# Seven products in place of eight for four of 22 gate and up blocks of a feed-forward stage

## The chip, the cores and the metric

The kernel runs on one core of a Trainium2 chip, whose engines work side by side: TensorE (PE, with its weight loads shown as PEld) multiplies, VectorE (DVE) and ScalarE (ACT) work on elements, GpSimd (POOL) is nearly unused here, SyncE (SP) issues the loads. The metric is device microseconds for one execution; lower is better. Every execution computes the whole of the reference from arrays in the chip's main memory.

## The reference

Two layers over 256 tokens with 1024 features, float32. Each layer is a feed-forward stage, a mixing stage and a second feed-forward stage, each added to x. So there are four feed-forward stages, which are what the change is about:

```python
def swiglu(h, w_gate_up, w_down):
    a, b = jnp.split(h @ w_gate_up, 2, axis=-1)
    return (jax.nn.silu(a) * b) @ w_down

x = x + 0.5 * swiglu(rms_norm(x, ffn1_norm), ffn1_w_gate_up, ffn1_w_down)
h = rms_norm(x, mix_norm)
# mixing: pooling over windows of 2, 4, 8, 16 tokens and causal attention, gated and merged
x = x + merged @ w_out
x = x + 0.5 * swiglu(rms_norm(x, ffn2_norm), ffn2_w_gate_up, ffn2_w_down)
```

The hidden width is 2816, 22 blocks of 128 features. w_gate_up has 1024 rows and 5632 columns, w_down 2816 rows and 1024 columns. rms_norm multiplies each token by one factor (the reciprocal root of its mean square) and each feature by a gain.

## The kernel before

**Precision.** Every float32 operand is split into two float32r parts, hi (a rounded copy, made by ScalarE) and lo (the rest, made by VectorE). A product is hi x hi, hi x lo and lo x hi, added up in PSUM. With the activations as the moving operand, one matmul streams 512 columns (hi and lo of 256 tokens) past the hi weights, and a second streams the 256 hi columns past the lo weights: `chain` (L136). Where the weights move and the activations stand (`tokens`, L369, for q, k and v in the mixing stage), a k-step of 128 rows is four matmuls of 512, 256, 512 and 256 columns.

**Weights.** They arrive in units of 1 MB, 128 partitions x 2048 columns. `fetch` (L96) loads one into a "raw" tile (four buffers) through SyncE's queue and splits it in two halves of 1024 columns into "hi" and "lo" tiles (six buffers each, so three units); `unit` (L90) hands the oldest one out. A gate and up unit holds one block of 128 gate features and the matching 128 up features, for all eight k-blocks of 128 rows: unit[p, k, gate or up, 128].

**A feed-forward stage** (`ffn`, L296). The gain is multiplied into x while it is split (`split_x`, L224, into "hx"); the factor per token is computed beside the first blocks (`factor_spread`, L276) and multiplied in later. For each of 22 blocks `pair` (L154) runs 8 x 2 chains into a PSUM tile of the pool "mm" (two buffers), then `drain` adds the two column halves (one copy on ScalarE, one add on VectorE) into "ab". A block or more later "ab" is scaled by the token factor (L340, VectorE), ScalarE takes the Silu of the gate half (L344), VectorE multiplies (L345), and `halves` (L187) splits the result into the tiles "ga", "gc" and "gb" (8, 8 and 6 blocks). Then comes the down projection: eight output blocks, each with 22 chains over those tiles into a PSUM tile of the pool "at" (four buffers; L347 to L359), added to x by `add_x`.

**Order.** TensorE runs in the order in which the program is written (`mm` wraps every matmul with `keep`, L78). The other engines' instructions are put in order by a planner, which takes them by their place in the program as soon as their operands and buffers are free; `behind` (L169) pins one behind another. Each engine then runs its own instructions strictly in that order.

The first stage of the first layer starts while its weights still arrive and has its own code (`n0`); the other three take the `else` branch at L320. In the mixing stage the tiles "gc" and "gb" hold other things (L482 to L488).

Of the kernel before, what the change touches and what calls it, by code (L numbers as in the profile page):

```python
# [18 lines left out]
F32 = mybir.dt.float32  # L19
# [23 lines left out]


C_G1, C_GM, C_G2, C_BG, C_PS, NG = 0, 8, 16, 24, 40, 44


@with_exitstack
def trunk_kernel(ctx: ExitStack, tc: tile.TileContext, x_in, w_in, pw_in, qkn_in, rope_in, mask_in, band_in, out):
# [28 lines left out]
    def mm(*args, **kw):  # L78
        return keep(nc.tensor.matmul(*args, **kw))  # L79
# [5 lines left out]

    n_unit = [0]

    ahead = []

    def unit():  # L90

        if not ahead:
            fetch()
        return ahead.pop(0)

    def fetch(last=None):  # L96

        raw, hi, lo = buffers()
        u = n_unit[0]
        n_unit[0] += 1  # L100
        n = HALF if u < 4 else 2 * HALF
        for c in range(0, 2 * HALF, n):
            nc.sync.dma_start(raw[:, c:c + n], w_in[u, :, c:c + n])
# [6 lines left out]
    def buffers():  # L110
        raw = raws.tile([P, 2 * HALF], F32, name="raw", tag="raw")
# [19 lines left out]

    def prod(ps, w, xk, first, last):

        return mm(steps(ps), lhsT=w, rhs=steps(xk), start=first, stop=last)

# [80 lines left out]
    for t in range(PAD - 1):  # L216
        g = min(g for g, w in enumerate(WINDOWS) if t < w - 1)
        nc.gpsimd.memset(inv[:, g:, t:t + 1], 1.0 / (t + 1))

    hx = acts.tile([P, NK, 2, S], F32R, name="hx")  # L220
    hk = [hx[:, k] for k in range(NK)]
# [45 lines left out]
    def spread(dr, st):  # L267
# [6 lines left out]
        return r  # L274

    def factor_spread():  # L276

# [17 lines left out]

    def ffn(after, n0=0, end=False):  # L296
        gs = []
        for n, m in (("ga", 8), ("gc", 8), ("gb", NF - 16)):
            g = acts.tile([P, m, 2, S], F32R, name=n, tag=n)
            gs.extend(g[:, i] for i in range(m))  # L300
        abs_ = []

        def wide():
            if n0 and len(abs_) in range(5, 13):
                ab = acts.tile([P, 2, S], F32, name="ab", tag="gates", bufs=NK)
            else:
                ab = tmp.tile([P, 2, S], F32, name="ab", tag="t512", bufs=5)
            abs_.append((len(abs_), ab))
            return abs_[-1][1]

        r = []

        def sums():
            r.append(factor_spread())

        if n0:
            pairs([unit() for _ in range(n0)], [wide() for _ in range(n0)])
            pair(unit(), wide(), sums, NK // 2)
            fetch()
        else:  # L320
            ws = [unit() for _ in range(2)]
            ts = [wide() for _ in range(2)]
# [3 lines left out]
            drain(ts[0], pss[0])  # L326
            sums()
            columns(ws[1], pss[1], range(4, NK))
            drain(ts[1], pss[1])
        done = 0  # L330
        for i in range(n0 + 1 if n0 else 2, NF + 1):
            if i < NF:
                pair(unit(), wide())
                fetch()

            todo = range(done, min(done + (2 if not n0 or i % 3 == 2 else 1), i) if i < NF else NF)
            done = todo.stop
            for j in todo:
                ab = abs_[j][1]
                scaled = tt(ab, ab, bc2(r[0]), op=OP.mult)  # L340
# [3 lines left out]
                act(sg, ab[:, 0, :], AF.Silu)  # L344
                tt(sg, sg, ab[:, 1, :], op=OP.mult)  # L345
                halves(gs[j], sg)
        for b in range(NK * NF):  # L347
# [129 lines left out]
    def mix(l, after):  # L477
# [7 lines left out]
        spare = acts.tile([P, 8 * GW], F32, name="spare", tag="ga")  # L485
        ax = acts.tile([P, 8, 2, S], F32R, name="ax", tag="gc")
        yk, pk = ([ax[:, i] for i in range(a, a + 4)] for a in (0, 4))
        qk = acts.tile([P, 12, S], F32, name="qk", tag="gb")  # L488
# [229 lines left out]
    for f in range(NK):  # L718
        square_x(f)
    n_unit[0] = len(w3)  # L720
    ahead.extend(w[1:] for w in w3)
    for l in range(L):
        ffn(lambda f: prep(f, l, C_GM), len(w3) if l == 0 else 0)
        if l == 0:
            for d, z in ((rope, rope_in), (mask, mask_in), (qkn, qkn_in)):
                nc.sync.dma_start(d, z)
        mix(l, lambda f: prep(f, l, C_G2))
        if l + 1 < L:
            ffn(lambda f: prep(f, l + 1, C_G1))
        else:  # L730
            ffn(lambda f: nc.sync.dma_start(out[:, f, :], x[:, f, :]), end=True)

# [89 lines left out]
```

## Time and profile before

| What | Value |
|---|---|
| Runs | 1004.05 us (median of 3: 1003.82, 1004.05, 1006.15) |
| Span of the profiled execution | 1001.7 us; the page states no time of its own for it |
| TensorE, matmuls | 996.8 us busy |
| VectorE, ScalarE | 788.9 and 619.0 us busy |
| Granted TensorE clock | 1.00 of full speed in all 40 slices |
| Loads | 192.89 MB, mean 193 GB/s |

The span runs from the first to the last instruction; a run's time has some more around it. A row of a group reads: line of the code, engine, operation, output tile and input tiles, shape, count, busy time and mean ns of one, then the idle time of that engine just ahead of these instructions and what ended it. A row of the chain reads: start, duration, engine and tile, number of instructions. The three stages that the change touches begin at 326, 502 and 822 us of the span (48 matmuls of 0.167 us ahead of the factor's "ss" matmuls at 334.25, 510.50 and 829.89).

### The profile page before, as it was taken

The page shows a single profiled execution, that of the slowest core. Times are in us where ns is not written, and L with a number is a line of the kernel's source. Part 1 is how long each engine was busy: PE and PEld are TensorE (multiplying, and loading weights), DVE is VectorE, ACT ScalarE, POOL GpSimd, SP SyncE. Part 2 cuts the span into 40 slices and gives each one's busy share as a digit, 9 for nine tenths or more (in the row PEclk, how much of TensorE's full clock was granted, in tenths as well). Part 3 has the DMA queues.
Part 4 walks back from the last instruction along what each step waited for, and adds up shares of the span by engine and source line. Part 5 has one row for each costly group of instructions (what it writes and reads, how often), then busy time and mean ns, then how long its engine had stood idle before and what let it go on. Part 6 is the DMA issues. An engine that isn't in the chain of part 4 may idle for free.

```text
span 1001.7 us, 16029 instructions
## 1 busy us (share of the span) xinstructions
PE 996.8 (100%) x6348; PEld 905.8 (90%) x6348; DVE 788.9 (79%) x1175; ACT 619.0 (62%) x981; POOL 16.1 (2%) x46
## 2 busy tenths in 40 slices
PE   9999999999999999999999999999999999999998
PEld 8899888898899988999988888889989999989988
DVE  6998866698978888886688888666988888888752
ACT  7866655557756666665576666556677567666541
POOL 0000000002000000000000000000020000000000
PEclk9999999999999999999999999999999999999999
DMA  8866655643546665565556566555544465565640
GB/s 290 318 210 210 210 183 196 220 156 137 187 152 211 208 212 173 206 210 191 192 189 213 183 209 203 185 202 190 185 178 171 134 215 202 190 203 196 207 150 22
DMA packets 30170, 192.89 MB, mean 193 GB/s; under 512 B 3344, under 2 KB 4624, under 8 KB 7568
## 3 DMA queue, kind: packets, MB, share of 16 engines
q1 hardware_dynamic: 30096, 191.88, 55.8%
q8 instruction: 49, 0.80, 0.3%
q14 instruction: 25, 0.20, 0.1%
HBM read 190.82 MB, written 1.05 MB: 192 GB/s over the span
## 4 chain that ended last, share of the span: by engine, by line
PE 99%; DMA 0%; DVE 0%; ACT 0%; SPq 0%; issue 0%
PE ps L79 84%; PE pt L79 7%; PE two L79 4%; PE pe L79 1%; PE sc L79 1%; PE pt L463 1%; PE y L79 1%; DMA raw<-w 0%; PE tp L419 0%; PE st L79 0%; PE ss L79 0%; DVE gx L367 0%; ACT hi L117 0%; SPq L708 0%
## 5 line engine op out<-in xcount | busy, mean ns | idle before, releaser
L79 PE MATMUL ps<-hx,hi 128*128 128x512 f32 x1696 | 568.5, 383 | 0.5 <-ACT hi L117 0.5
L118 DVE TENSOR_TENSOR lo<-raw,hi 128x1024 fp32r<-128x1024 f32 (+2 forms) x372 | 441.1, 1192 | 137.9 <-ACT hi L117 133.1
L117 ACT ACTIVATE hi<-raw 128x1024 fp32r<-128x1024 f32 (+2 forms) x372 | 380.8, 1030 | 230.4 <-PE ps L79 175.8
L79 PE MATMUL ps<-hx,lo 128*128 128x256 f32 x1696 | 463.4, 273 | 0.0
L79 PEld LDWEIGHTS ps<-hx,hi 128*128 128x128 f32 x1696 | 318.4, 188 | 57.6 <-ACT hi L117 0.8
L79 PEld LDWEIGHTS ps<-hx,lo 128*128 128x128 f32 x1696 | 318.7, 188 | 0.2 <-DVE lo L118 0.2
L79 PE MATMUL ps<-ga,hi 128*128 128x512 f32 (+1 forms) x264 | 87.0, 376 | 0.0
L79 PE MATMUL ps<-gc,hi 128*128 128x512 f32 (+1 forms) x264 | 87.0, 376 | 0.0
L79 PE MATMUL ps<-ga,lo 128*128 128x256 f32 x256 | 69.9, 273 | 0.0
L79 PE MATMUL ps<-gc,lo 128*128 128x256 f32 x256 | 69.9, 273 | 0.0
L79 PE MATMUL ps<-gb,hi 128*128 128x512 f32 (+1 forms) x198 | 65.6, 376 | 0.0
L79 PE MATMUL pt<-hi,hx 128*128 128x512 f32 x192 | 64.9, 384 | 0.0
L340 DVE TENSOR_TENSOR ab<-ab,r 128x512 f32<-128x512 f32 x88 | 60.3, 690 | 2.2
L167 DVE TENSOR_TENSOR ab<-ps,ab 128x512 f32<-128x512 f32 x86 | 59.0, 686 | 2.0
L79 PEld LDWEIGHTS ps<-ga,hi 128*128 128x128 f32 x264 | 49.0, 188 | 8.3
L79 PEld LDWEIGHTS ps<-gc,hi 128*128 128x128 f32 x264 | 49.0, 188 | 8.3
L79 PE MATMUL pt<-lo,hx 128*128 128x256 f32 x192 | 52.5, 274 | 0.0
L344 ACT ACTIVATE sg<-ab 128x256 f32<-128x256 f32 x88 | 36.2, 417 | 26.4 <-DVE ab L340 24.8
L79 PE MATMUL ps<-gb,lo 128*128 128x256 f32 x192 | 52.4, 273 | 0.0
L166 ACT ACTIVATE ab<-ps 128x512 f32<-128x512 f32 x86 | 49.9, 580 | 0.0
L79 PEld LDWEIGHTS ps<-gc,lo 128*128 128x128 f32 x256 | 48.1, 188 | 0.0
L79 PEld LDWEIGHTS ps<-ga,lo 128*128 128x128 f32 x256 | 48.1, 188 | 0.0
(150 smaller groups left out, 1018.9 us busy)
## 6 DMA issues: line engine op xcount, KB each, us to landing
raw<-w SPq DMA_DIRECT2D x176, 1024.0 KB, 5.0
raw<-w SPq DMA_DIRECT2D x16, 256.0 KB, 5.3
out_dram<-gx SPq DMA_DIRECT2D x8, 128.0 KB, 2.0
gx<-x SPq DMA_DIRECT2D x3, 256.0 KB, 6.3
qk<-pw SPq DMA_DIRECT2D x2, 256.0 KB, 2.7
gx<-x SPq DMA_DIRECT2D x1, 300.0 KB, 2.9
qkn<-qkn SPq DMA_DIRECT2D x1, 256.0 KB, 5.2
rope<-rope SPq DMA_DIRECT2D x1, 128.0 KB, 5.0
```

The lines of the kernel that those rows point to most:

```text
L79: return keep(nc.tensor.matmul(*args, **kw))
L117: act(hi, w, AF.Copy)
L118: return tt(lo, w, hi.bitcast(F32), op=OP.subtract)
L166: act(t, ps[:, :, 1, :], AF.Copy)
L167: drained.append(tt(t, ps[:, :, 0, :], t, op=OP.add))
L340: scaled = tt(ab, ab, bc2(r[0]), op=OP.mult)
L344: act(sg, ab[:, 0, :], AF.Silu)
L463: keep(nc.tensor.transpose(pt[:, h, o * P:(o + 1) * P], pr[:, h, c * P:(c + 1) * P], ident))
```

## The change

Blocks 12 to 15 of three feed-forward stages are no longer multiplied one by one. Their 256 gate and up columns each make a matrix of 1024 columns, cut in two by two blocks: W11 and W12 (rows 0 to 511; blocks 12, 13 and blocks 14, 15), W21 and W22 (rows 512 to 1023). The activations with the gain are cut in two by two as well, by 128 tokens and by 512 features. The four result blocks then come from seven products of (128 tokens x 512) by (512 x 512) in place of eight, by a scheme of Strassen's kind.

- The order of weights is a list, `feed_order`: blocks 0 to 4, then one of the seven forms ahead of each of the blocks 5 to 11, then blocks 16 to 21.
- `sum_form` makes a form of the weights. Forms 1, 2 and 3 are plain loads (W11 into the tile "sa", W21 into a raw tile, W22 into a part of the tile "pre"). Forms 5, 6 and 4 add W12, W22 and W21 to "sa" in turn, and form 7 adds W12 to "pre": these four are loads that add, issued by GpSimd. Each form is 1 MB and is split like a unit.
- `x_forms`, behind the drain of block 2, makes four sums of the activations and splits them; three products take parts of "hx" as they are.
- `by_tokens` multiplies: activations stand, weights move, four matmuls per k-step as in `tokens`. The result has tokens on the partitions.
- `strassen` sums the products and gates them (`gated`), with the token factor as a scalar per partition; `factor_tokens` computes it so at the stage's start, from two matmuls of one column.
- `turned` transposes the gated blocks on TensorE, two blocks of features at a time, behind blocks 11 and 16, and splits them into the tile "gd", which takes half of what was "gc".

Nothing changes in the first stage, the down projection and the mixing stage, but that "gc" is now two tiles there too.

```diff
+GROUP = 12
+FIRST = 5
+FORMS = {
+    "1": ("a", False, "11"), "2": ("c", False, "21"), "5": ("a", True, "12"), "3": ("b", False, "22"),
+    "6": ("a", True, "22"), "7": ("b", True, "12"), "4": ("a", True, "21"),
+}
+def feed_order():
+    z, forms = [], list(FORMS)
+    for n in (*range(GROUP), *range(GROUP + 4, NF)):
+        if n >= FIRST and forms:
+            z.append(forms.pop(0))
+        z.append(n)
+    return z
+def feed_units(base):
+    return [base + n if isinstance(n, int) else (base, n) for n in feed_order()]
...
+    plan = []
+    for base in (0, FU, LU, LU + FU):
+        plan.extend(feed_units(base) if base else range(NF))
+        plan.extend(range(base + NF, base + NF + NF // 2))
+        if base in (0, LU):
+            plan.extend(range(base + NF + NF // 2, base + FU))
...
+        u = next(plan)
+        if isinstance(u, tuple):
+            ahead.append(sum_form(*u))
...
+    def sum_form(base, f):
+        n = base + GROUP
+        q = {"11": (n, 0), "12": (n + 2, 0), "21": (n, 1), "22": (n + 2, 1)}
+        at, add, src = FORMS[f]
+        if at == "c":
+            sums_at["c"] = raws.tile([P, 2 * HALF], F32, name="raw", tag="raw")
+        z = sums_at[at].rearrange("p (i c) -> p i c", i=2)
+        u, kh = q[src]
+        w = w_in[u:u + 2, :, kh * HALF:(kh + 1) * HALF].rearrange("u p c -> p u c")
+        if add:
+            nc.gpsimd.dma_start(z, w, accum_op=OP.add)
+        else:
+            nc.sync.dma_start(z, w)
+        _, hi, lo = buffers(False)
+        z = z.rearrange("p i (k c) -> p i k c", c=2 * P)
+        for h in range(2):
+            a = z[:, :, 2 * h:2 * h + 2, :]
+            hv, lv = (t[h].rearrange("p (k i c) -> p i k c", i=2, c=2 * P) for t in (hi, lo))
+            act(hv, a, AF.Copy)
+            tt(lv, a, hv.bitcast(F32), op=OP.subtract)
+        return hi, lo
...
+    def factor_tokens():
+        st = quarter("st")[:, 0, :2]
+        for t in range(2):
+            mm(st[:, t:t + 1], lhsT=acc[:, t * P:(t + 1) * P], rhs=ones[:, :1], start=True, stop=True)
+        rt = small.tile([P, 2], F32, name="rt", tag="rt", bufs=2)
+        rsqrt(rt, st, 1.0 / D)
+        nt = small.tile([P, 2], F32, name="nt", tag="nt", bufs=1)
+        nc.vector.tensor_scalar(nt, rt, -1.0, None, op0=OP.mult)
+        return rt, nt
...
+        def post(n):
+            ab = abs_[n]
+            scaled = tt(ab, ab, bc2(r[0]), op=OP.mult)
+            sg = small.tile([P, S], F32, name="sg", tag="sg", bufs=2)
+            act(sg, ab[:, 0, :], AF.Silu)
+            tt(sg, sg, ab[:, 1, :], op=OP.mult)
+            halves(gs[n], sg)
+            return scaled
...
+            sums_at["a"] = acts.tile([P, 2 * HALF], F32, name="sa", tag="gd")
+            pre = acts.tile([P, 12 * S], F32, name="pre", tag="gb")
+            sums_at["b"] = pre[:, :NK * S]
+            xg = pre[:, :NK * S].rearrange("p (k s) -> p k s", s=S)
+            vt = acts.tile([P, 2, GW], F32, name="vt", tag="v")
+            tk = [acts.tile([P, 2, GW], F32, name="tk", tag="tok", bufs=2) for _ in range(2)]
+            p1, p5, c12 = tk[0][:, 0], tk[0][:, 1], tk[1][:, 0]
+            gq = {tn: vt[:, tn // 2, tn % 2 * S:(tn % 2 + 1) * S] for tn in range(4)}
+            sf = {}
+            def x_forms():
+                late = drained[-1]
+                for k in range(NK):
+                    behind(act(xg[:, k, :], x[:, k, :], AF.Copy, scale=gain[:, l_of[0], col + k:col + k + 1]), late)
+                a11, a21 = (xg[:, :4, t * P:(t + 1) * P] for t in range(2))
+                a12, a22 = (xg[:, 4:, t * P:(t + 1) * P] for t in range(2))
+                s1, s2 = (pre[:, (8 + 2 * i) * S:(10 + 2 * i) * S].rearrange("p (k s) -> p k s", s=P) for i in range(2))
+                s3, s4 = (vt[:, i, :].rearrange("p (k s) -> p k s", s=P) for i in range(2))
+                tt(s1, a22, a21, op=OP.subtract)
+                stt(s2, s1, -1.0, a11, op0=OP.mult, op1=OP.subtract)
+                tt(s3, a11, a21, op=OP.subtract)
+                stt(s4, s2, -1.0, a12, op0=OP.mult, op1=OP.subtract)
+                for n, z in (("5", s1), ("3", s4), ("6", s2), ("7", s3)):
+                    sh, sl = (acts.tile([P, 4, P], F32R, name="sf", tag="gates", bufs=NK) for _ in range(2))
+                    act(sh, z, AF.Copy)
+                    tt(sl, z, sh.bitcast(F32), op=OP.subtract)
+                    sf[n] = [(sh[:, k, :], sl[:, k, :]) for k in range(4)]
+                for n, k0, t in (("1", 0, 0), ("2", 4, 0), ("4", 4, 1)):
+                    sf[n] = [tuple(hx[:, k, j, t * P:(t + 1) * P] for j in range(2)) for k in range(k0, k0 + 4)]
+            def by_tokens(f, ps, first):
+                hi, lo = unit()
+                more = {} if first else {"skip_group_check": True}
+                for k, (ah, al) in enumerate(sf[f]):
+                    wh, wl = blk(hi, 4 * k, 4), blk(lo, 4 * k, 4)
+                    prod(ps, ah, wh, first and k == 0, False, **more)
+                    prod(ps[:, :S], ah, wl[:, :S], False, False, **more)
+                    prod(ps, al, wh, False, False, **more)
+                    prod(ps[:, S:], ah, wl[:, S:], False, k == 3, **more)
                 fetch()
-            todo = range(done, min(done + (2 if not n0 or i % 3 == 2 else 1), i) if i < NF else NF)
-            done = todo.stop
-            for j in todo:
-                ab = abs_[j][1]
-                scaled = tt(ab, ab, bc2(r[0]), op=OP.mult)
-                if n0 and i == n0 + 1:
-                    behind(scaled, drained[-1])
+            def gated(c, t, n, sign):
+                c = c.rearrange("p (i j s) -> p i j s", i=2, j=2)
+                sc = r[1][sign][:, t:t + 1]
                 sg = small.tile([P, S], F32, name="sg", tag="sg", bufs=2)
-                act(sg, ab[:, 0, :], AF.Silu)
-                tt(sg, sg, ab[:, 1, :], op=OP.mult)
-                halves(gs[j], sg)
+                act(by_half(sg), c[:, :, 0, :], AF.Silu, scale=sc)
+                stt(by_half(gq[2 * t + n]), c[:, :, 1, :], sc, by_half(sg), op0=OP.mult, op1=OP.mult)
+            def turned(n):
+                pt = quarter("pt")
+                for i in range(2):
+                    for t in range(2):
+                        keep(nc.tensor.transpose(pt[:, i, t * P:(t + 1) * P], gq[2 * t + n][:, i * P:(i + 1) * P], ident))
+                g = gt[2][:, 2 * n:2 + 2 * n]
+                act(g[:, :, 0, :], pt, AF.Copy)
+                tt(g[:, :, 1, :], pt, g[:, :, 0, :].bitcast(F32), op=OP.subtract)
+            bank = {}
+            def strassen(f):
+                b = {"1": "a", "2": "a", "5": "e", "3": "e", "6": "g", "7": "f", "4": "f"}[f]
+                fresh = b not in bank
+                if fresh:
+                    bank[b] = quarter("p" + b).rearrange("p a s -> p (a s)")
+                z = bank[b]
+                by_tokens(f, z, fresh)
+                if f == "1":
+                    act(p1, z, AF.Copy)
+                elif f == "2":
+                    gated(z, 0, 0, 0)
+                elif f == "5":
+                    act(p5, z, AF.Copy)
+                elif f == "6":
+                    tt(p1, z, p1, op=OP.add)
+                    tt(c12, bank["e"], p1, op=OP.add)
+                    gated(c12, 0, 1, 1)
+                elif f == "7":
+                    tt(p5, z, p5, op=OP.add)
+                    tt(p5, p5, p1, op=OP.add)
+                    gated(p5, 1, 1, 1)
+                elif f == "4":
+                    tt(p1, z, p1, op=OP.add)
+                    gated(p1, 1, 0, 0)
+            late = []
+            wait = [0, 1]
+            for i, n in enumerate(feed_order()[2:]):
+                if isinstance(n, str):
+                    strassen(n)
+                    if n in "74":
+                        late.append([2, 1 if n == "7" else 0])
+                    continue
+                pair(unit(), wide(n))
+                fetch()
+                if i == 0:
+                    x_forms()
+                for m in wait[:2]:
+                    post(m)
+                wait = wait[2:] + [n]
+                if n == GROUP - 1:
+                    room("gd", 4)
+                    room("gb", NF - 16)
+                for z in late:
+                    z[0] -= 1
+                    if z[0] == 0:
+                        turned(z[1])
+            for m in wait:
+                post(m)
         for b in range(NK * NF):
             f, k = divmod(b, NF)
             if b % 16 == 0:
...
```

More of the change, by code (lines that the diff above doesn't have):

```diff
@@ L108, in fetch, with buffers @@
         ahead.append((hi, lo))
-    def buffers():
-        raw = raws.tile([P, 2 * HALF], F32, name="raw", tag="raw")
+    sums_at = {}
+    def sum_form(base, f):
[19 more added lines that the diff above has]
+        return hi, lo
+    def buffers(raw=True):
+        raw = raws.tile([P, 2 * HALF], F32, name="raw", tag="raw") if raw else None
         hi = [parts.tile([P, HALF], F32R, name="hi", tag="hi") for _ in range(2)]
@@ L130, in steps, with prod @@
         return z.rearrange("p (s a c) -> p a s c", a=4, c=4)
-    def prod(ps, w, xk, first, last):
-        return mm(steps(ps), lhsT=w, rhs=steps(xk), start=first, stop=last)
+    def prod(ps, w, xk, first, last, **kw):
+        return mm(steps(ps), lhsT=w, rhs=steps(xk), start=first, stop=last, **kw)
     def chain(ps, hi, lo, b, xk, first, last):
@@ L294, in bc2, with ffn, room, wide @@
         return a.unsqueeze(1).to_broadcast([P, 2, a.shape[-1]])
-    def ffn(after, n0=0, end=False):
-        gs = []
-        for n, m in (("ga", 8), ("gc", 8), ("gb", NF - 16)):
+    def ffn(after, n0=0, end=False, col=None):
+        gs, gt = [], []
+        def room(n, m):
             g = acts.tile([P, m, 2, S], F32R, name=n, tag=n)
+            gt.append(g)
             gs.extend(g[:, i] for i in range(m))
-        abs_ = []
-        def wide():
+        room("ga", 8)
+        room("gc", 4)
+        abs_ = {}
+        def wide(n):
             if n0 and len(abs_) in range(5, 13):
-                ab = acts.tile([P, 2, S], F32, name="ab", tag="gates", bufs=NK)
+                abs_[n] = acts.tile([P, 2, S], F32, name="ab", tag="gates", bufs=NK)
             else:
-                ab = tmp.tile([P, 2, S], F32, name="ab", tag="t512", bufs=5)
-            abs_.append((len(abs_), ab))
-            return abs_[-1][1]
+                abs_[n] = tmp.tile([P, 2, S], F32, name="ab", tag="t512", bufs=5)
+            return abs_[n]
         r = []
@@ L314, in sums @@
             r.append(factor_spread())
-        if n0:
-            pairs([unit() for _ in range(n0)], [wide() for _ in range(n0)])
-            pair(unit(), wide(), sums, NK // 2)
-            fetch()
+            if not n0:
+                r.append(factor_tokens())
+        def post(n):
[6 more added lines that the diff above has]
+            return scaled
+        if n0:
+            room("gd", 4)
+            room("gb", NF - 16)
+            ws = [unit() for _ in range(n0)]
+            pairs(ws, [wide(n) for n in range(n0)])
+            pair(unit(), wide(n0), sums, NK // 2)
+            fetch()
+            done = 0
+            for i in range(n0 + 1, NF + 1):
+                if i < NF:
+                    pair(unit(), wide(i))
+                    fetch()
+                todo = range(done, min(done + (2 if i % 3 == 2 else 1), i) if i < NF else NF)
+                done = todo.stop
+                for n in todo:
+                    scaled = post(n)
+                    if i == n0 + 1:
+                        behind(scaled, drained[-1])
         else:
             ws = [unit() for _ in range(2)]
-            ts = [wide() for _ in range(2)]
             pss = [banks(pmm, "ps") for _ in range(2)]
@@ L485, in mix @@
         spare = acts.tile([P, 8 * GW], F32, name="spare", tag="ga")
-        ax = acts.tile([P, 8, 2, S], F32R, name="ax", tag="gc")
-        yk, pk = ([ax[:, i] for i in range(a, a + 4)] for a in (0, 4))
+        yk, pk = ([z[:, i] for i in range(4)] for z in (
+            acts.tile([P, 4, 2, S], F32R, name=n, tag=t) for n, t in (("yk", "gc"), ("pk", "gd"))))
         qk = acts.tile([P, 12, S], F32, name="qk", tag="gb")
@@ L719, in trunk_kernel @@
         square_x(f)
-    n_unit[0] = len(w3)
+    for _ in w3:
+        next(plan)
     ahead.extend(w[1:] for w in w3)
     for l in range(L):
-        ffn(lambda f: prep(f, l, C_GM), len(w3) if l == 0 else 0)
+        l_of[0] = l
+        ffn(lambda f: prep(f, l, C_GM), len(w3) if l == 0 else 0, col=C_G1)
         if l == 0:
```

23 lines of the change are left out of this document (12 added, 11 removed).

## The prediction

> **What bounds the kernel now.** I read the page's busy line first, then the chain of waits in order of time, then the groups of one stretch, and last the queues. The busy line and the chain's summary:
>
> ```profile
> PE 996.8 (100%) x6348; PEld 905.8 (90%) x6348; DVE 788.9 (79%) x1175; ACT 619.0 (62%) x981; POOL 16.1 (2%) x46
> PE 99%; DMA 0%; DVE 0%; ACT 0%; SPq 0%; issue 0%
> ```
>
> TensorE sets the end: the chain never leaves it for longer than the first load. So time comes off only where TensorE gets fewer columns, and any wait put ahead of a matmul is paid in full. The chain in order of time gives what a matmul costs (start, us, what, how many):
>
> ```profile
> 182.86 10.96 PE pt L79 x64
> 193.82 0.34 PE st L79 x4
> 194.16 10.78 PE pt L79 x64
> 204.94 0.34 PE st L79 x2
> 205.28 10.68 PE pt L79 x64
> 215.96 0.87 PE tp L419 x8
> 216.83 10.67 PE ps L79 x64
> ...
> 334.25 0.23 PE ss L79 x2
> 334.47 176.02 PE ps L79 x1056
> ```
>
> The last row is a whole feed-forward stage without a gap: 1056 matmuls in 176.02 us, 166.7 ns each (a 512-column and a 256-column one alternate). A gate and up block is 16 pairs, so 32 x 0.1667 = 5.33 us. The row starts in the middle of block 1 (the "ss" matmuls stand there), so block 1 ends at 334.47 + 16 x 0.1667 = 337.14, block 4 at 353.1, block 6 at 363.8.
>
> How near VectorE and ScalarE are to a bound is read in the same stage, blocks 4 to 21 (window, length, busy of PE, PEld, DVE, ACT, POOL, clock, DMA share, GB/s; then VectorE's and ScalarE's groups there):
>
> ```profile
> 350.00:446.00 96.00, 96.00 (x578) 86.38 (x577) 80.43 (x111) 59.96 (x90) 0.00 (x0) 1.00 0.59 200
> ```
> ```profile
> L118 DVE TENSOR_TENSOR lo<-raw,hi 128x1024 fp32r<-128x1024 f32 x37 | 45.3, 1223 | 10.9 <-ACT hi L117 9.8
> L167 DVE TENSOR_TENSOR ab<-ps,ab 128x512 f32<-128x512 f32 x19 | 13.0, 687 | 0.6
> L340 DVE TENSOR_TENSOR ab<-ab,r 128x512 f32<-128x512 f32 x18 | 12.4, 692 | 0.6
> L345 DVE TENSOR_TENSOR sg<-sg,ab 128x256 f32<-128x256 f32 x18 | 7.5, 418 | 0.0
> ...
> ```
> ```profile
> L117 ACT ACTIVATE hi<-raw 128x1024 fp32r<-128x1024 f32 x36 | 38.0, 1054 | 19.1 <-PE ps L79 19.1
> L166 ACT ACTIVATE ab<-ps 128x512 f32<-128x512 f32 x18 | 10.4, 580 | 0.0
> L344 ACT ACTIVATE sg<-ab 128x256 f32<-128x256 f32 x18 | 7.6, 420 | 5.7 <-DVE ab L340 5.6
> ...
> ```
>
> 96 us are 18 blocks: VectorE works 80.43 / 18 = 4.47 us of each 5.33, ScalarE 3.33. VectorE is the second engine, with 0.86 us to spare per block; ScalarE waits for TensorE to give weight buffers back (19.1 us), so splits run as far ahead as the buffers allow. How far, by VectorE's and ScalarE's timelines:
>
> ```profile
> 350.42 1.06 ACT L117 ACTIVATE hi<-raw 128x1024 fp32r<-128x1024 f32 x1 [0.82 <-PE ps L79]
> ```
> ```profile
> 350.93 0.68 DVE L340 TENSOR_TENSOR ab<-ab,r 128x512 f32<-128x512 f32 x1
> 351.53 1.22 DVE L118 TENSOR_TENSOR lo<-raw,hi 128x1024 fp32r<-128x1024 f32 x1
> ```
>
> At 350.42 block 4's first half has just been used up. Three units fit the buffers, so this split is for block 7, which starts at 363.8: it is done at 352.75, a **lead** of 11.0 us.
>
> **The change part by part.** All terms are per stage, three stages.
>
> Products. Removed: four blocks, 128 matmuls, 128 x 0.1667 = 21.33 us. Added: seven products of 4 k-steps with 2 x (512 + 256) columns, 112 matmuls in the form that "pt" has (activations stationary, weights moving). The trace has that form at 10.96, 10.78 and 10.68 us for 64, mean 10.81 or 168.9 ns each: 112 x 0.1689 = 18.91 us. **Gain 2.42 us**; with 10.96 (19.18 for 112) it is 2.15, with the "ps" rate of 10.67 (18.67) it is 2.66. I take the mean, the three rows being the same code with the same operands as the products.
>
> Added on TensorE: eight 128x128 transposes ("turned"), 0.87 us by the "tp" row, and two one-column matmuls with the scale per token ("factor_tokens"), 0.34 us by the "st" x4 row. Both stand in TensorE's program order, so nothing covers them: **loss 1.21 us**. The transposes come two blocks after their product (at least 5.33 + 5.33 us behind it), and what they wait for (two sums, a Silu, a multiplication) is below 3 us of work by the 0.69 and 0.42 us groups, so I cost that wait at nothing; without the cover it would be those 3 us.
>
> Net on TensorE 2.42 - 1.21 = 1.21 us per stage, 3.6 us in all.
>
> VectorE and ScalarE. The four blocks lose their drains and gating, but seven forms are split in place of four units. Over the stretch in which a form stands ahead of each of blocks 5 to 11, TensorE takes 7 x 5.33 + 18.91 = 56.2 us. VectorE needs 7 x 4.47, plus 7 forms x 2 x 1.223, plus five 512-wide sums at 0.69 and four 256-wide multiplications at 0.42 from the "strassen" branches: 31.3 + 17.1 + 5.1 = 53.5 us. It fits, with 2.7 us left. But "x_forms" comes before it, behind the drain of block 2: eight 512-wide operations at 0.69 (5.5 us), and five tiny ones of the scale per token (the tiny ones of the token scale last 0.16 each):
>
> ```profile
> L252 DVE SCALAR_TENSOR_TENSOR rt<-a,rt 128x2 f32<-128x2 f32 x2 | 0.3, 161 | 0.1
> ```
>
> That is 6.3 us, against 3 x 0.86 = 2.6 to spare in blocks 2 to 4: the stretch begins 3.7 us late on VectorE. With a form between blocks, three units of buffers are worth 5.33 - 2.7 = 2.6 us less, so the lead is 11.0 - 2.6 = 8.4 us. 3.7 is below 8.4: **I cost it at nothing, hidden by the lead**, and with the lead gone it would be 3.7 us per stage. ScalarE: x_forms adds eight 256-wide scaled copies (the split of the activations shows 0.50) and four 512-wide (0.58), 6.3 us, against 3 x 2.0 spare; in the stretch 7 x (3.33 + 2.11) + 2 x 0.58 + 4 x 0.42 = 40.9 of 56.2.
>
> ```profile
> L227 ACT ACTIVATE hx<-gx 128x256 fp32r<-128x256 f32 x48 | 23.6, 499 | 6.8 <-DVE gx L367 3.6 <-DVE gx L696 1.7 <-DMA gx<-x 1.3
> ```
>
> PSUM. A second product of a bank waits until the first was read out (form 2 behind the copy of 1, form 3 behind that of 5, form 4 behind the sum of 7). A block of 5.33 us stands between each two; the copy takes 0.58, the sum 0.69. Nothing, unless the queue of that engine is 4.6 us late.
>
> Loads. Seven 1 MB transfers replace four; four of them add into a tile and come from GpSimd's queue, which is idle in these stages. SyncE's queue:
>
> ```profile
> SPq L103 <- DVE lo L118: 540.5, 117, 16.2
> SPq L103 <- DVE sg L345: 218.3, 34, 6.5
> ```
> ```profile
> raw<-w SPq DMA_DIRECT2D x176, 1024.0 KB, 5.0
> ```
> ```profile
> DMA to landing us min/median/max: 4.1/5.0/10.5
> ```
>
> SyncE waits for buffers, not for memory. Two new waits stand in it: form 1 waits until the tile "gd" is free of the stage before, form 3 until x_forms has read "pre"; the block loads behind each wait too. A load is issued when the raw tile four units before has been split, some 6 units before its use, and by its landing of 5.0 us (10.5 at worst) it has over 15 us in hand: nothing. Form 5 waits, on GpSimd, for the split of form 1 (both use tile "sa"), 6 for 5, 4 for 6. Between two uses of the tile stand two blocks and two forms, 16.1 us of TensorE; the split itself takes 1.05 + 2 x 1.22 = 3.5, so an adding load has 12.6 us before it delays a split, and the lead on top. The trace has no adding load. From below it is a plain one, 5.0; from above, one that moves its bytes twice through what the others leave: 0.59 of the engines carry 200 GB/s, so all carry 339, and the other 0.41 carry 139; 2.1 MB at 139 GB/s are 15.1 us, and 1.9 of start and landing (5.0 less 1.05 MB at 339) make 17.0. I take a value below 12.6, as the nearest row is the plain load: nothing.
>
> [...]
>
> **Sum:** span 1001.7 less 3.6 is 998.1. The page gives no time of its own for the profiled execution; the runs' median, 1004.05, lies 2.35 above the span, so the forecast is **1000.4 us**. Its own range goes by the product rate: gain 2.15 gives 3 x 0.94 = 2.8 and 1001.2, gain 2.66 gives 3 x 1.45 = 4.4 and 999.7.
>
> **The rivals.**
>
> A, small stalls take the gain. The lo half waits for the hi half of the same weights (9.8 us of waits in the window above), so the two engines' lateness may add instead of overlap: ScalarE's 6.3 us of x_forms ahead of the next hi half and VectorE's 3.7 behind it make 10.0 against a lead of 8.4, 1.6 us per stage, 4.8 in all: 1005.2; with half of it 1002.8. For it: both engines get their extra work at one place. Against: the splits of the next two units are already done when it starts. It would be within 0.3%.
>
> B, slower: the adding loads are late. Three follow each other on one tile; with 17.0 us each is 4.4 late, together 13.2, less the lead of 8.4, 4.8 us per stage: 1000.4 + 14.4 = 1014.8. It decides from 12.6 + 8.4 / 3 = 15.4 us per load. For it: the 10.5 us worst plain load, and that ScalarE, waiting for the load, keeps the drains of finished blocks behind it. Against: GpSimd and 0.41 of the DMA engines are free.
>
> C, slower: VectorE becomes the bound in the stretch. In the window it idles 96 - 80.4 = 15.6 us, over 18 units 0.87 each. If this idle time belongs to each split, the 14 units of the stretch need 53.5 + 12.2 = 65.7 us for TensorE's 56.2; 9.5 + 3.7 - 8.4 = 4.8 per stage: 1014.8 too. Against: the idle time is there because the buffers are full, and goes when VectorE is behind.
>
> D, the change doesn't gain what it says: all products at the slowest "pt" rate or a little slower, and the waits of the transposes not covered by 0.5 us a stage: 1001.2 + 1.5 = 1002.7, within 0.3%.
>
> **How the numbers follow.** A measurement of this kernel can tell 0.3%, 3.0 us, from no change: faster is below 1001.0, slower above 1007.1. Forecast 0.44, A 0.22, D 0.08, B 0.12, C 0.14. Faster 0.45 (forecast, and a little of A with stalls near nothing), same 0.30, slower 0.25. The range goes from 999.2 (the forecast's lower end, less half of the three 0.34 us, since the "st" row also holds the change to the next tile) up to 1010: it holds the forecast, A, D and the small half of B and C (stalls of half the worked size, 1007.6). The forecast's own range is 999.7 to 1001.2.
>
> **What would show it.** In the changed kernel's chain: per stage 128 matmuls less of "ps" and 112 more of the new form; a stage with 1.2 us less from its "ss" row to the next stage's; eight transposes at 0.87. Right: TensorE's busy share stays at 99 to 100% and its waits stay below 1 us. A shows as waits of TensorE for hi or lo of the units just behind x_forms. B shows as ScalarE waiting for a transfer at the splits of forms 5, 6, 7, 4, and landing times above 15 us. C shows as VectorE at 95% or more from block 5 to 11 and TensorE waiting for lo. D shows as more than 169 ns per matmul of the products. Wrong altogether: a TensorE clock below 1.00, or stalls in stages that have no products.

## The result and the profile after

The changed kernel takes 1010.21 us (median of 6 runs, 1007.77 to 1013.67) beside 1003.93 us for the kernel before (6 runs, 1003.43 to 1006.15): a ratio of 1.0063, 95% interval 1.0043 to 1.0082. It is 0.6% slower where 0.4% faster was forecast. The profiled execution took 1010.54 us, with a span of 1008.8. The six runs of the changed kernel lie 5.9 us apart, at mean granted TensorE clocks of 0.997 to 1.000 that do not put them in order.

The busy line and the summary of the chain, from the page of the changed kernel:

```profile
PE 997.2 (99%) x6336; PEld 904.4 (90%) x6336; DVE 808.9 (80%) x1217; ACT 641.5 (64%) x1026; POOL 30.6 (3%) x58
PE 81%; DMA 9%; DVE 4%; ACT 3%; issue 2%; SPq 0%; ACTq 0%; POOLq 0%
```

No engine is overloaded on average; VectorE rose from 79% to 80%. But the chain (the work that ended last, followed back step by step), which was TensorE alone before, now runs 9% of the span through DMA, and through VectorE and ScalarE behind it. Where it leaves TensorE is read in the chain in order of time (start, us, what):

```profile
334.73 0.34 PE st L103 x4
335.07 18.79 PE ps L103 x112
...
353.91 8.95 DMA sa<-w
...
369.67 10.99 DMA sa<-w
...
384.83 12.48 DMA sa<-w
...
397.42 1.06 ACT hi L163
...
404.12 0.61 DVE tk L510
...
404.87 4.57 PE pf L103 x16
409.44 5.47 PE ps L103 x32
414.91 0.44 PE pt L484 x4
...
584.16 2.92 PE pf L103 x16
...
905.27 2.90 PE pf L103 x16
```

(The row of 112 at 335.07 is the rest of block 1 and blocks 2 to 4; the 112 matmuls of the products come after it.) In the first and the third changed stage the chain goes through the three adding loads of tile "sa" (forms 5, 6 and 4), in the second through form 5's and then that of "pre" (form 7). From there it goes through ScalarE and VectorE, and in all three it comes back to TensorE at product 4 ("pf"). The groups of waits of the whole execution (us in total, times, longest) say what stood still:

```profile
ACT hi L163 <- DMA sa<-w: 26.9, 9, 3.7
ACT hi L163 <- DMA pre<-w: 9.7, 3, 4.3
PE pf L103 <- DVE tk L510: 6.2, 3, 2.4
```

ScalarE waited 36.6 us for the twelve adding loads, 12.2 per stage, and TensorE waited once per stage, 2.4 us at most, for the sum "tk" of product 7. The loads themselves (KB each, us to landing; L155 issues the POOLq ones):

```profile
raw<-w SPq DMA_DIRECT2D x167, 1024.0 KB, 4.9
sa<-w POOLq DMA_DIRECT2D x9, 1024.0 KB, 10.0
pre<-w POOLq DMA_DIRECT2D x3, 1024.0 KB, 13.0
```

How a wait of ScalarE becomes one of TensorE is seen in the two timelines of the first such place (start, us, engine, line, what; in brackets the idle time ahead and what ended it). ScalarE's:

```profile
397.42 1.06 ACT L163 ACTIVATE hi<-sa 128x1024 fp32r<-128x1024 f32 x1 [3.32 <-DMA sa<-w]
...
400.09 1.05 ACT L163 ACTIVATE hi<-sa 128x1024 fp32r<-128x1024 f32 x1
401.04 0.57 ACT L223 ACTIVATE ab<-ps 128x512 f32<-128x512 f32 x1
```

VectorE's:

```profile
399.65 1.22 DVE L164 TENSOR_TENSOR lo<-sa,hi 128x1024 fp32r<-128x1024 f32 x1
...
401.17 1.23 DVE L164 TENSOR_TENSOR lo<-sa,hi 128x1024 fp32r<-128x1024 f32 x1
402.31 0.68 DVE L224 TENSOR_TENSOR ab<-ps,ab 128x512 f32<-128x512 f32 x1
402.91 1.21 DVE L175 TENSOR_TENSOR lo<-raw,hi 128x1024 fp32r<-128x1024 f32 x1
404.04 0.68 DVE L510 TENSOR_TENSOR tk<-pf,tk 128x512 f32<-128x512 f32 x1
```

Product 7 ended on TensorE at 396.93, so its sum (L510) could have run then. In VectorE's order it stands behind both lo halves of form 4, the drain of block 9 (which had ended at 394.18) and another lo half. The lo halves need ScalarE's hi halves, and these wait for the load. So the sum runs at 404.04, 7.1 us after its operands were there. Product 4 accumulates into the same PSUM bank and may not start before the sum has read it; between product 7 and product 4 stands one block of 5.35 us. 7.1 less (5.35 - 0.68) is 2.4 us, and that is the gap in the trace: TensorE has nothing from 402.43 to 404.87. In the other two stages it is 1.8 and 1.9 us. Form 4 itself was there in time.

The longest gap cost more than its length. The stretch behind it (window, length, busy of PE, PEld, DVE, ACT and POOL, clock, DMA share, GB/s):

```profile
402.50:409.28 6.78, 4.41 (x16) 3.83 (x17) 6.78 (x10) 4.51 (x8) 0.00 (x0) 0.75 0.18 37
```

The granted clock is 0.75 there, and product 4 took 4.57 us; behind the gaps of 1.8 and 1.9 it took 2.92 and 2.90. The three gaps make 6.2 us, the slow product 1.7 more: 7.9 us, about the distance from the changed kernel to the versions below that have no gap (1001.7 to 1002.5).

### The profile page after: what moved, and what is told of

It is laid out like the page before. It is cut to its first block, busy times and chain, and to the rows that moved or that the text cites. A ratio compares the mean times of both kernels' runs of the same rounds, so it can differ in the third digit from the quotient of the medians.

```text
span 1008.8 us, 16140 instructions
## 1 busy us (share of the span) xinstructions
PE 997.2 (99%) x6336; PEld 904.4 (90%) x6336; DVE 808.9 (80%) x1217; ACT 641.5 (64%) x1026; POOL 30.6 (3%) x58
## 4 chain that ended last, share of the span: by engine, by line
PE 81%; DMA 9%; DVE 4%; ACT 3%; issue 2%; SPq 0%; ACTq 0%; POOLq 0%
PE ps L103 65%; DMA sa<-w 7%; PE pt L103 7%; PE two L103 4%; DVE lo L164 1%; DMA pre<-w 1%; PE pe L103 1%; DVE lo L175 1%; PE pf L103 1%; PE sc L103 1%; ACT hi L163 1%; ACT pre L442 1%; PE pt L657 1%; DVE ab L224 1%; PE y L103 1%
## 5 line engine op out<-in xcount | busy, mean ns | idle before, releaser
L103 PE MATMUL ps<-hx,hi 128*128 128x512 f32 x1504 | 506.9, 384 | 0.9 <-ACT hi L174 0.9
L175 DVE TENSOR_TENSOR lo<-raw,hi 128x1024 fp32r<-128x1024 f32 (+2 forms) x348 | 411.1, 1189 | 111.5 <-ACT hi L174 109.2
L174 ACT ACTIVATE hi<-raw 128x1024 fp32r<-128x1024 f32 (+2 forms) x348 | 352.8, 1026 | 180.0 <-PE ps L103 128.5
L103 PE MATMUL ps<-hx,lo 128*128 128x256 f32 x1504 | 411.0, 273 | 0.0
L103 PEld LDWEIGHTS ps<-hx,hi 128*128 128x128 f32 x1504 | 282.4, 188 | 51.8 <-ACT hi L174 1.2
L103 PEld LDWEIGHTS ps<-hx,lo 128*128 128x128 f32 x1504 | 282.6, 188 | 0.3 <-DVE lo L175 0.3
L163 ACT ACTIVATE hi<-sa 128x1024 fp32r<-128x1024 f32 x24 | 25.3, 1052 | 30.3 <-DMA sa<-w 26.9
L103 PE MATMUL ps<-gc,hi 128*128 128x512 f32 (+1 forms) x132 | 44.3, 376 | 0.0
L103 PE MATMUL ps<-gd,hi 128*128 128x512 f32 (+1 forms) x132 | 44.3, 376 | 0.0
L103 PE MATMUL ps<-mk,hi 128*128 128x256 f32 x256 | 44.1, 275 | 0.0
```

What stands on the lines that cost most here:

```text
L163: act(hv, a, AF.Copy)
L174: act(hi, w, AF.Copy)
L175: return tt(lo, w, hi.bitcast(F32), op=OP.subtract)
```

## The experiments

What had to be explained was the wait of product 4, and that even without it the time would stand at 1002, not 1000.4. Theory 1 was formed from the trace after: the adding loads land in 8.4 to 13.9 us, ScalarE stands still at the split that waits for them, and the drains and sums behind that split in the in-order queues of ScalarE and VectorE come late. Its rivals: that the order in which the planner laid these queues is the cause and the loads are only what it is stretched by; that the extra work of `x_forms` had used up the lead, whatever the loads do; and that GpSimd's queue, not the addition, makes the loads slow. The ratios are to the kernel before, run beside each of them.

**Loads that do not add.**

```diff
         if add:
-            nc.gpsimd.dma_start(z, w, accum_op=OP.add)
+            nc.gpsimd.dma_start(z, w)
```

> The four adding loads per stage are issued as plain loads, same queue, same tile, same order of instructions on every engine; the weights of forms 5, 6, 7 and 4 are then single quarters, not sums, so the output is not the reference's. Theory 1 (the adding loads land 9 to 13 us after their issue, ScalarE stands still for them in its fixed order, and everything behind it gets late): landings near 5 us, ScalarE's wait for these loads falls from 12.6 us in the first changed stage to under 3, TensorE's wait for the sum of product 7 (6.2 us in three stages) is gone, time about 1002 us. Rival 2 (the order alone puts that sum too late, whatever the loads do): the wait stays at 2 us per stage, time 1007 to 1010. Rival 3 (the work of x_forms puts both engines behind): also 1007 to 1010.

Measured 1002.24 us (11 runs) beside 1003.81 (29 runs): 0.9983 (0.9974 to 0.9992). The five engines have the same instructions in the same order as the changed kernel. From its page and its waits:

```profile
sa<-w POOLq DMA_DIRECT2D x9, 1024.0 KB, 5.7
pre<-w POOLq DMA_DIRECT2D x3, 1024.0 KB, 5.5
```

```profile
ACT hi L163 <- DMA sa<-w: 1.8, 2, 1.5
```

The same bytes from the same queue land in 5.7 and 5.5 us instead of 10.0 and 13.0, ScalarE's 36.6 us of waiting become 1.8, and TensorE's wait is gone. So the addition makes the loads long, not the queue; and with the order unchanged, short loads suffice to remove the stall.

**The same loads, another order.** The first split of an adding form is pinned behind the drain of an earlier block.

```diff
-            act(hv, a, AF.Copy)
+            first = act(hv, a, AF.Copy)
+            if add and h == 0:
+                behind(first, drained[-2])
```

> Only the order is changed: the first half split of each form that is made by an adding load is put behind the drain of the block that is two blocks back. Theory 1: the loads still land 9 to 13 us after issue, but fewer instructions stand behind the wait; TensorE's wait for the sum of product 7 goes below 1 us per stage, time 1002 to 1004. Rival 2: the wait is gone as well, 1002 to 1004. Rival 3: the wait stays, 1007 to 1010.

Measured 1001.90 us (9 runs): 0.9977 (0.9967 to 0.9986). The loads land in 11.6 and 13.0 us, no sooner than before, but ScalarE waits for them 12.0 us in place of 36.6, in shorter pieces:

```profile
ACT hi L163 <- DMA sa<-w: 8.7, 7, 2.1
ACT hi L163 <- DMA pre<-w: 3.3, 3, 1.5
```

VectorE's timeline at the same place shows the sum of product 7 between the two lo halves of form 4, 6 us sooner than in the changed kernel:

```profile
396.73 1.23 DVE L166 TENSOR_TENSOR lo<-sa,hi 128x1024 fp32r<-128x1024 f32 x1
397.87 0.68 DVE L512 TENSOR_TENSOR tk<-pf,tk 128x512 f32<-128x512 f32 x1
398.47 1.22 DVE L166 TENSOR_TENSOR lo<-sa,hi 128x1024 fp32r<-128x1024 f32 x1
```

TensorE doesn't wait. Long loads alone are no stall either; they need an order that puts a drain or a sum behind the wait.

**Without x_forms.** Its sums and splits are left out; products 5, 3, 6 and 7 multiply parts of "hx".

```diff
                 if i == 0:
-                    x_forms()
+                    for fm, k0, t in (("1", 0, 0), ("2", 4, 0), ("4", 4, 1), ("5", 0, 1), ("3", 4, 0), ("6", 0, 0), ("7", 4, 1)):
+                        sf[fm] = [tuple(hx[:, k, j, t * P:(t + 1) * P] for j in range(2)) for k in range(k0, k0 + 4)]
```

> x_forms is left out: no sums of the activations are made, products 5, 3, 6 and 7 take parts of hx in their place, so the output is not the reference's. Adding loads as in the changed kernel. Rival 3: no backlog, TensorE's wait gone, 1001 to 1003, and ScalarE no longer waits for the adding loads. Theory 1: the first adding load is issued some 5 us sooner (348 in place of 353.9 us of the first changed stage), but each still lands 9 to 13 us after issue and ScalarE waits for it, 6 us per stage or more; TensorE's wait for the sum of product 7 is smaller than 2 us per stage but the time stays above 1003. Rival 2: 1007 to 1010.

Measured 1001.73 us (11 runs): 0.9978 (0.9969 to 0.9986). The stall is gone here too, with loads of 11.0 and 11.1 us:

```profile
ACT hi L163 <- DMA sa<-w: 6.5, 4, 3.3
ACT hi L163 <- DMA pre<-w: 1.5, 2, 0.8
```

Theory 1 had expected more than 1003. So the loads are not enough by themselves: without the work of x_forms (on VectorE 345.75 to 354.7 in the changed kernel, eight operations between the usual ones) the splits are earlier and the first adding load is issued at 349.84 in place of 353.91. The planner also lays the queues anew when the work is gone, and that part is not separated.

**Form 4's splits behind the sum of product 7, on both engines.**

```diff
+            first = act(hv, a, AF.Copy)
+            low = tt(lv, a, hv.bitcast(F32), op=OP.subtract)
+            if f == "4" and h == 0:
+                behind(first, sum7[-1])
+                behind(low, sum7[-1])
```

> Only the order is changed: the split of form 4 stands behind the sum of product 7 on ScalarE and VectorE. Rival 2: TensorE's wait is gone, 1002 to 1003. Theory 1: the sum is no longer behind the wait for the last load, but the split of form 4 now comes later and TensorE waits for hi or lo of form 4 instead, 1 to 2 us per stage, time 1005 to 1010.

Measured 1006.82 us (9 runs): 1.0026 (1.0016 to 1.0035). The wait for the sum is gone, and TensorE waits for the lo halves of form 4 themselves:

```profile
PE pf L103 <- DVE lo L165: 1.9, 2, 1.0
```

So putting the sum ahead by itself passes part of the stall on to the split: 1006.82 is still 4.6 us above the kernel with plain loads, where the changed kernel is 8.0 above it. What repairs it is the place of every adding form's split, as in the order above.

**The work of x_forms twice, with plain loads, and with the pinned order.** The sums and the splits of x_forms run twice; the first kernel has loads that do not add, the second the pinned order with adding loads.

```diff
-                tt(s1, a22, a21, op=OP.subtract)
...
+                for _ in range(2):
+                    tt(s1, a22, a21, op=OP.subtract)
...
-                    act(sh, z, AF.Copy)
-                    tt(sl, z, sh.bitcast(F32), op=OP.subtract)
+                    for _ in range(2):
+                        act(sh, z, AF.Copy)
+                        tt(sl, z, sh.bitcast(F32), op=OP.subtract)
```

> Plain loads in place of the adding ones, and the sums and splits of x_forms are made twice: 5.5 us more on VectorE and 2.3 us more on ScalarE at the place of x_forms in each stage. The weights of forms 5, 6, 7 and 4 are single quarters, so the output is not the reference's. Theory 1 (lateness of the two sources adds up, and the adding loads are the larger part): twice the work alone stays below the lead, no wait of TensorE over 1 us per stage, 1002 to 1003. Rival 3 (the work is what matters): TensorE waits again, 1.5 us per stage or more, 1006 or more.

> Adding loads, their first half split behind the drain two blocks back, and the sums and splits of x_forms made twice. It shows how much lateness the pinned order still bears. Theory 1: the added 5.5 us delay the split of form 1 and so the first adding load by about as much; the chain of three loads on one tile takes what is left of the lead, TensorE waits 0 to 2 us per stage, 1002 to 1008. Rival 3: 1006 or more, as in the kernel with plain loads and twice the work.

Measured 1014.75 us (4 runs; 1.0107, 1.0093 to 1.0120) and 1016.19 us (4 runs; 1.0114, 1.0100 to 1.0128). Both stall at the same new place, though one has short loads and the other a good order. The first one's wait and its chain:

```profile
PE ps L103 <- DVE lo L175: 8.2, 3, 2.7
```

```profile
357.98 1.15 DVE lo L175
359.12 0.04 issue
359.17 7.02 PE ps L103 x31
```

```profile
356.00:368.00 12.00, 9.28 (x46) 7.91 (x45) 11.05 (x16) 8.14 (x15) 0.00 (x0) 0.86 0.74 262
```

TensorE waits 2.7 us for the lo half of block 5, before any adding load matters, and then runs at a clock of 0.86 over that stretch. Theory 1 had expected 1002 to 1003 for the kernel with plain loads and at most 1008 for the other; both missed, and rival 3 was right that enough work alone makes TensorE wait.

How much lead x_forms leaves can be read in the timelines: when the lo half of block 5 is made, and when TensorE multiplies by it (the second matmul of the block). In the changed kernel:

```profile
355.25 1.22 DVE L175 TENSOR_TENSOR lo<-raw,hi 128x1024 fp32r<-128x1024 f32 x1
356.66 0.28 PE L103 MATMUL ps<-hx,lo 128*128 128x256 f32 x1
```

and in the kernel without x_forms:

```profile
349.38 1.22 DVE L175 TENSOR_TENSOR lo<-raw,hi 128x1024 fp32r<-128x1024 f32 x1
358.49 0.28 PE L103 MATMUL ps<-hx,lo 128*128 128x256 f32 x1
```

Without x_forms the lo half is ready 7.9 us before its use, with it 0.2 us, in all three stages. So the prediction's lead of 8.4 us was nearly right, but the lateness is 7.7 us and not 3.7. The eight operations make 4.8 us of it, at 0.60 from one to the next; VectorE waited 1.2 us for ScalarE's scaled copies, and most of the rest are three operations of earlier blocks that now stand ahead of this split. With the work doubled, five of the eight added operations stand ahead of it, 3.0 us, and 2.7 of these reach TensorE.

**x_forms two blocks later.**

```diff
-                if i == 0:
+                if n == 4:
                     x_forms()
```

> x_forms behind the drain of block 4 in place of block 2, adding loads and order otherwise by the planner. Theory 1 with the start of the chain as the cause: the split of form 1 is no longer behind x_forms, the first adding load is issued at about 349 us of the span in place of 353.9, ScalarE's waits for these loads fall below 6 us per stage and TensorE's wait goes below 1 us per stage, 1002 to 1004. If the backlog of VectorE and ScalarE decides, wherever it arises: the wait stays at 2 us per stage or grows, 1007 to 1012.

Measured 1015.47 us (4 runs): 1.0115 (1.0100 to 1.0131), worse than the changed kernel.

```profile
ACT hi L163 <- DMA sa<-w: 27.9, 5, 6.6
PE pf L103 <- DVE tk L510: 7.6, 3, 3.3
```

The first adding load is issued sooner (347.62), but the second only at 369.43, as late as before (369.67), for x_forms now stands between the two splits. So an earlier start of the loads' row is of no use by itself. That the lateness of the two engines decides, when the waits begin, fits this; the expectation that said so had 1007 to 1012, and the stall is larger than that.

**The pinned order, and the token factor without matmuls.** The two one-column matmuls of `factor_tokens` are replaced by a multiplication with the identity and a row sum on VectorE.

```diff
-        for t in range(2):
-            mm(st[:, t:t + 1], lhsT=acc[:, t * P:(t + 1) * P], rhs=ones[:, :1], start=True, stop=True)
+        tt(dg, r.rearrange("p (a b) -> p a b", b=P), bc2(ident), op=OP.mult)
...
-        rsqrt(rt, st, 1.0 / D)
+        nc.vector.tensor_reduce(rt, dg, axis=AX.X, op=OP.add)
```

> The pinned kernel, with the factor per token taken out of the spread factor on VectorE (a multiplication with the identity and a sum over each row) in place of two one-column matmuls and the root on two columns. Both theories: no wait of TensorE, and 0.34 us per stage less on it: 1.0 us below the pinned kernel, 1000.9.

> The pinned kernel with the factor from VectorE once more, beside the one with the extra matmuls: 1000.7, and below the pinned kernel by about 1.0.

> The pinned kernel once more on the same chip as the two others: 1001.9. Where products and blocks are fast and slow is as in its first profile if this is set by the order of the instructions, and differs if it is set by chance.

Measured 1000.66 us (5 runs; 0.9969, 0.9956 to 0.9981) and, run again, 1000.78 (7 runs; 0.9975, 0.9964 to 0.9985). The pinned order alone, run again, took 1002.48 (11 runs; 0.9987, 0.9978 to 0.9996). This is the best version found: 0.3% below the kernel before. Against the pinned order it is 1.2 and 1.7 us, where three times 0.34 us of "st" matmuls make 1.0. The 112 matmuls behind "st" are faster too when it is gone, 18.69 us in place of 18.77 in the chains of the first changed stage.

**Why no version without a stall reaches 3.6 us.** Two executions of the pinned order show it in the chain of the first changed stage. The first run:

```profile
364.16 5.49 PE ps L103 x32
...
385.97 2.67 PE pg L103 x16
...
402.29 2.67 PE pf L103 x16
```

and the repetition of the same kernel:

```profile
393.58 2.75 PE pf L103 x16
396.33 5.35 PE ps L103 x32
```

Once the products take 2.67 us (166.9 ns a matmul) and the blocks behind them 5.49 (171.6); once the products take 2.75 (171.9) and the blocks 5.35. Each execution has both: in the first run the second and third changed stage are as in the other fence, in the repetition the third stage has 2.67 and 5.49. The program is the same, so the order of the instructions alone doesn't set which it is. A product with its block takes 8.10 or 8.16 us; the prediction's terms, 18.91 / 7 + 5.33, make 8.03. Seven of these are 0.5 or 0.9 us per stage more than worked; with two stages of the one and one of the other they make 1.9 us, and 1.7 and 2.2 are missing (3.6 forecast, 1.9 and 1.4 measured). The slower rate, a pair in 342 ns in place of 333, was measured here in stretches where the two forms of matmul alternate, in either of them. The kernel before has both rates too: its three "pt" rows of 64 took 10.96, 10.78 and 10.68, which the prediction averaged. A last kernel put a matmul of four columns of zeros behind each product of the best version, to see whether the switch can be absorbed there.

```diff
                     prod(ps[:, S:], ah, wl[:, S:], False, k == 3, **more)
+                mm(ps[:, :4], lhsT=one_r, rhs=zero_r, start=False, stop=True, skip_group_check=True)
```

> The pinned kernel with the factor from VectorE, and behind each of the seven products one more matmul of 4 columns, which adds zeros to the product's bank. In the kernels without stalls the same pair of a 512-column and a 256-column matmul runs at 333 ns in some stretches and at 342 in others, and which it is changes where products and blocks follow each other: the six blocks between products take 5.49 us each in the pinned kernel, the later products 2.67. If the rate is set by how one stretch follows another and not by the operands, the extra matmul changes which stretches are slow: products or blocks flip between 2.67 and 2.75 or 5.33 and 5.49. If it belongs to the kind of matmul or to what VectorE, ScalarE and the loads do beside it, each block and each product keeps the time it has without the extra matmul. The extra matmuls cost about 0.1 us each, 2 us in all: 1002 to 1003 if nothing flips, 1000.5 if all blocks become fast.

Measured 1002.37 us (11 runs; 0.9987, 0.9978 to 0.9995), 1.6 us more than without it. From its chain:

```profile
393.66 2.75 PE pf L103 x17
396.41 5.45 PE ps L103 x32
```

Product and block are now 8.20 us: the matmul costs 0.1 us each time and absorbs nothing. What sets the rate stays open.

## Why the prediction was wrong, step by step

**Products.** Gain 2.42 us per stage, by 18.91 for seven: at 2.67 and 2.75 each, as in the two fences above, seven take 18.7 and 19.2, and the seven blocks behind them 1.1 and 0.1 us more than worked. The sum had no term for this rate; with it the gain is 1.5 and 1.9.

**Transposes and token factor.** Loss 1.21 us: 0.44 + 0.44 for "pt" and 0.34 for "st", as worked. The wait of the transposes was indeed nothing.

**x_forms, "hidden by the lead".** Failed by its size. The lateness was reckoned at 3.7 us and the lead at 8.4; 7.7 and 7.9 were measured. Nothing was still the right price at blocks 5 to 7, where TensorE did not wait, but by 0.2 us at block 5. But the 8.4 - 3.7 = 4.7 us that were to be left were not there for what came next. VectorE could not catch up soon either: in the kernel with plain loads it is busy for 54.71 of the 56.68 us from product 1 to block 11 (53.5 of 56.2 had been worked).

**Adding loads, "nothing".** This is the step that failed most. The landing times were inside its bounds (8.4 to 13.9 us, in 5.0 to 17.0), and seven of the nine of "sa" were below the 12.6 us allowed, so by its own rule, with the lead on top, nothing should have come of them. But the lead had been used up, and the 12.6 were counted from one use of the tile on TensorE to the next, and the split doesn't wait there: in ScalarE's order it stands as far ahead as the planner put it, and the whole of ScalarE, then VectorE's lo half, waits with it. The slack of a load is the time until the first instruction that waits for it comes to the head of its queue, not until its data are used. The plain load, chosen as the nearest row, was also about half of what was measured.

The adding loads took 10.0 us ("sa") and 13.0 ("pre") to land, in the median, beside 5.7 and 5.5 for plain loads of the same queue: a factor of 1.8 and 2.4. What the addition does in that time no run here shows.

**PSUM, "nothing, unless the queue of that engine is 4.6 us late".** The condition was the right one and it held: the queue was 7.1 us late at the sum of product 7, and 7.1 less 4.7 is the gap. It was written down as a condition and not followed up to a price.

**Rivals.** A's lateness of 10.0 against a lead of 8.4 was nearer to the 7.7 and 7.9 measured than the forecast's 3.7, but its stall just behind x_forms did not come. B named the mechanism ("ScalarE, waiting for the load, keeps the drains of finished blocks behind it") and its sign; its deciding point of 15.4 us per load was wrong, since loads of 8.4 to 13.9 were enough, and so was its place, which was not form 4 but the sum in front of it. Its price, 4.8 us per stage, was above the 2.1 of gap that were measured. C is refuted by the kernel with plain loads: there VectorE is busy for 97% of the stretch (the 54.71 us above), over C's sign of 95%, and TensorE doesn't wait; in the changed kernel it is busy for 53.66 of 61.06 us, 88%. D's figure is near what is left when the stall is removed, 1002.7 worked and 1001.9 and 1002.5 measured, in part by luck: products at the slowest "pt" rate are what some stages show, and blocks at that rate, which it didn't name, the others, while the 1.5 us that it adds for the waits of the transposes did not come.

The measured 1010.2 lies 0.2 above the range's upper end. The clock below 1.00 had been named as what would be wrong altogether, and no term stood for it; it came behind the longest gap, at 0.75 in the mean from 402.50 to 409.28, and made 1.7 us in the profiled execution.

So three things together make the stall at product 4: the loads that add, the order of two in-order queues, and the work of x_forms ahead of them. Changing any one removes it (the first, second and third experiment; the third leaves open how much the queues' new order does). The loads and the work were each costed at nothing against the same lead, and the order had no price at all.

## What to carry to other kernels

When a slower transfer or a new wait is added to an engine with a fixed order, follow what stands behind the waiting instruction in that queue and in the queues that it feeds, and reckon the slack to the instruction's place in its queue, not to the use of the data. One lead covers one lateness: several costs that are each "hidden by the lead" have to be summed against it. What is left of a lead can be read off a trace, as the time from the end of a split to the first matmul that uses it. A term for products that replace others wants the rate of the two forms alternating, and not that of either alone: here 8.10 or 8.16 us for a product with its block, where the two rates apart make 8.03.

## What the runs showed of the hardware

A load of 1 MB that adds took 8.4 to 13.9 us to land in the changed kernel (median 10.0 for "sa", 13.0 for "pre") and 1.2 us of GpSimd to issue. A plain one on the same queue, in the kernel with loads that do not add, took 5.7 ("sa") and 5.5 ("pre") in the median, and 0.7 to issue.

Behind some short gaps of TensorE its granted clock was lower. In the changed kernel the gap of 2.4 us was followed, within 0.5 us, by five pairs of matmuls at 640 ns in place of 333 (a clock of 0.75 from 402.50 to 409.28, 1.7 us lost); behind those of 1.8 and 1.9 the clock was 1.00. In the kernel with x_forms doubled and plain loads the three gaps make 8.2 us and the longest is 2.7, so all are about as long; the clock was 0.86 from 356 to 368 us, where the first of them lies, and in one window of each of the other two changed stages it was 0.83 (540 to 550) and 1.00 (864 to 874). In the kernel with x_forms later, where the gaps go up to 3.3 us, product 4 of the first changed stage took 2.92 us, as behind the gap of 1.8. So the length alone does not seem to decide whether the clock falls; what does, no run here shows.

The same pair of matmuls ran at 333 or 342 ns. In the first run of the pinned order products and blocks took 2.67 and 5.49 us in the first changed stage, from the third product on, and 2.75 and 5.35 in the second and third stage; in the repetition the third stage had 2.67 and 5.49, from the second product on, and the first and second had 2.75 and 5.35. So which stage it is changed from one execution to the next. The cause is open.
